# Feed-forward gate and up products by Strassen's algorithm in an fp32 streaming trunk: seven half-block products for eight

## The chip, the cores and the metric

The kernel runs on one core of one Trainium2 chip. The metric is device time of one execution in microseconds; the time given for a kernel is the median of its runs. The matmuls run on TensorE (PE; its weight loads are PEld), element-wise work on VectorE (DVE), ScalarE (ACT) and GpSimd (POOL), and SyncE (SP) issues the transfers that bring weights from DRAM.

## The reference

A two-layer trunk over 640 token columns (512 of a prompt, 8 x 16 of samples), width 1024, all in fp32. Each layer adds a mixer (pooling and differential attention in layer 0, an RWKV-7 recurrence in layer 1), cross-attention over a memory of 256 rows, and a gated feed-forward part of width 2816:

```python
def rmsnorm(x, g):
    y = x32 * lax.rsqrt(jnp.mean(x32 * x32, axis=-1, keepdims=True) + NORM_EPS)
    return y * g
def swiglu(h, wg, wu, wd):
    return (jax.nn.silu(h @ wg) * (h @ wu)) @ wd
...
x = x + swiglu(rmsnorm(x, P['norm_ffn_g'][l]), P['ffn_wg'][l], P['ffn_wu'][l], P['ffn_wd'][l])
```

The change is in the feed-forward part alone, in both layers.

## The kernel before

Activations stay in SBUF transposed: `x` is 8 blocks of 128 features by 640 tokens, and a product goes over the tokens in two halves of 320 (`HALVES`), one PSUM bank each. An fp32 product is made of three fp32r ones: each operand is split into a high part (rounded by a cast) and a low part (the rest), and `block_steps` issues wh·xh, wh·xl, wl·xh for each of the 8 feature blocks and both halves, 48 matmuls for one block of 128 outputs.

Weights are streamed. `load_w` brings one block (128 x 1024 numbers, 512 KB) into `wr` by a transfer on SP's queue; ACT casts it to `wh`, and DVE subtracts to get `wl`. Each of the three kinds has two buffers, taken in turn (`wtile`).

`ffn` works without the normalisation at first: `normed` splits x·gain, and the factor 1/rms of each token (`rstd`) comes in when a product leaves PSUM. So the first products start while `rms` is still squaring, summing (matmuls with `ones`), taking root and reciprocal, and spreading the factor over the partitions (matmuls with the diagonal `dg`). The 22 hidden blocks go in groups of 8, 8 and 6. For each block f: the gate product; DVE multiplies it by `rstd`, ACT takes Silu; the up product; DVE multiplies by `rstd`, POOL multiplies gate by up, and ACT and DVE split the result into `hid`. After a group, a pass over `wd` (8 blocks) adds its part to x. The products turn through banks 0 to 5; banks 6 and 7 serve `rms` and, at the end of layer 0, the transposes of the memory rows (`mem_parts`).

A scheduler orders the instructions of each engine at build time, with a timeline that it simulates; on the chip each engine works through its own list in that order, and waits at an instruction until its inputs and its output's buffer are free. SBUF is cut into 56 wide slots (`NSLOT`) and 22 narrow ones (`NHALF`); every temporary takes a slot from a free list and rotates over as many as its ring has.

Of the kernel before, what the change touches and what calls it, by code (L numbers as in the profile page):

```python
# [9 lines left out]
F32 = mybir.dt.float32  # L10
F32R = mybir.dt.float32r
AF = mybir.ActivationFunctionType
ALU = mybir.AluOpType
# [8 lines left out]
NT = NP + NB * TS  # L22
NF = 22
HALVES = ((0, 320), (320, 320))
NEG = -1.0e30
EPS = 1e-6
NSLOT = 56
NHALF = 22
NSMALL = 32


# [8 lines left out]
class Trunk:  # L40
# [21 lines left out]
    def __init__(self, ctx, tc, io):  # L62
# [5 lines left out]
        self.dr = ctx.enter_context(tc.tile_pool(name="dr", bufs=1, space=DRAM))  # L68
        self.free = {"t": deque(range(NSLOT)), "n": deque(range(NHALF))}
        self.scopes = [{}]  # L70
# [54 lines left out]
    def take(self, k, name, kind="t", dt=F32):  # L125
        h = Held()
        h.slots = [(kind, self.pop(kind, name)) for _ in range(k)]
        h.extend(self.slot(kind, i, name, dt) for _, i in h.slots)
        return h
# [102 lines left out]

    def wtile(self, kind, dt):
        i = self.turn[kind]
        self.turn[kind] = (i + 1) % 2
        return self.wp.tile([128, 1024], dt, tag=f"{kind}{i}", name=kind, bufs=1)

    def load_w(self, src, kb, cols, rows=128):
# [795 lines left out]


    def ffn(self, l):
        nc, io = self.nc, self.io
        self.banks(g=(0, 1, 2, 3, 4, 5), r=(6, 7))
        wg, wu, wd = io["ffn_wg"][l], io["ffn_wu"][l], io["ffn_wd"][l]
        hl = self.normed(self.col["norm_ffn_g"][:, 8 * l:8 * l + 8])  # L1040
        first = [[self.load_w(self.wview(w, 0, 8, 0, 128), 8, 128)] for w in (wg, wu)]
        _, rstd = self.rms("r")
        r0 = rstd[0]
        for f0, nf in ((0, 8), (8, 8), (16, 6)):
            hid = self.hl(nf, "hid")
            with self.scope():
                for f in range(nf):
                    g = self.t("gate")[:, 0:NT]
                    sg = self.t("sgate")[:, 0:NT]

                    def ev_g(m, pts):
                        for p, (t0, n) in zip(pts, HALVES):
                            self.tt(g[:, t0:t0 + n], p, r0[:, t0:t0 + n])
                            self.act(sg[:, t0:t0 + n], g[:, t0:t0 + n], AF.Silu)

                    def ev_u(m, pts):
                        for p, (t0, n) in zip(pts, HALVES):
                            self.tt(g[:, t0:t0 + n], p, r0[:, t0:t0 + n])
                            self.tt(g[:, t0:t0 + n], g[:, t0:t0 + n], sg[:, t0:t0 + n], eng=nc.gpsimd)
                            self.split((hid[f][0][:, t0:t0 + n], hid[f][1][:, t0:t0 + n]), g[:, t0:t0 + n])  # L1060

                    self.gemm(hl, wg, 128, ev_g, c0=(f0 + f) * 128, first=() if f0 + f else first[0])
                    self.gemm(hl, wu, 128, ev_u, c0=(f0 + f) * 128, first=() if f0 + f else first[1])
            if f0 == 16:
                self.give(hl, rstd)
                if l == 0:
                    self.mem = self.mem_parts("r")
            self.gemm(hid, wd, 1024, self.add_x, r0=f0 * 128)
            self.give(hid)


    def rwkv(self):
# [890 lines left out]
```

## Time and profile before

| | |
|---|---|
| median of 3 runs | 2404.35 us (2401.02 to 2410.25) |
| profiled execution, its own time | 2405.84 us |
| its span | 2403.7 us |
| mean granted TensorE clock | 0.961 |
| PE busy | 2248.9 us (94%) |
| DVE busy | 1259.0 us (52%) |
| ACT busy | 820.4 us (34%) |
| POOL busy | 455.6 us (19%) |

The page of the profile gives the busy time of each engine and its share of the span. The feed-forward parts run from about 562 to 1025 us and from 1921 to 2383 us. The trace can be asked for the busy time of engines in any stretch, for groups of instructions (busy time, count, mean of one, idle time before them), for waits, and for a timeline in which neighbouring instructions of one kind are drawn together with their count. In it DVE's splits, adds and products all stand at L211 (`tt`), the fused gain-and-factor product at L214 (`stt`), matmuls at L230 (`mm`).

### The profile page before, as it was taken

The page shows a single profiled execution, that of the slowest core. Times are in us where ns is not written, and L with a number is a line of the kernel's source. Part 1 is how long each engine was busy: PE and PEld are TensorE (multiplying, and loading weights), DVE is VectorE, ACT ScalarE, POOL GpSimd, SP SyncE. Part 2 cuts the span into 40 slices and gives each one's busy share as a digit, 9 for nine tenths or more (in the row PEclk, how much of TensorE's full clock was granted, in tenths as well). Part 3 has the DMA queues.
Part 4 walks back from the last instruction along what each step waited for, and adds up shares of the span by engine and source line. Part 5 has one row for each costly group of instructions (what it writes and reads, how often), then busy time and mean ns, then how long its engine had stood idle before and what let it go on. Part 6 is the DMA issues. An engine that isn't in the chain of part 4 may idle for free. (4 is left out here: it accounts for less than half of the span.)

```text
span 2403.7 us, 45518 instructions
## 1 busy us (share of the span) xinstructions
PE 2248.9 (94%) x18933; PEld 2098.5 (87%) x18933; DVE 1259.0 (52%) x2197; ACT 820.4 (34%) x1513; POOL 455.6 (19%) x480
## 2 busy tenths in 40 slices
PE   8998899999999999989998886885999999999998
PEld 7886799889999999988887875664998899999998
DVE  3566433445433434485758785589435544244344
ACT  4335332334222212366745432222323432122122
POOL 1113220002101101245433110233100211011010
PEclk9999999999999999999998987897999999999998
DMA  3228445533222222353236666673445222222222
GB/s 118 75 75 298 147 144 158 172 93 88 79 71 79 71 85 75 113 167 115 80 109 162 162 175 155 174 196 106 145 133 170 67 71 79 77 74 79 80 73 77
DMA packets 428063, 280.41 MB, mean 117 GB/s; under 512 B 78873, under 2 KB 383278, under 8 KB 427857
## 3 DMA queue, kind: packets, MB, share of 16 engines
q1 hardware_dynamic: 424257, 268.01, 38.3%
q0 software_dynamic: 3600, 9.49, 1.1%
q8 instruction: 149, 2.44, 0.4%
q14 instruction: 57, 0.47, 0.1%
HBM read 231.22 MB, written 46.20 MB: 115 GB/s over the span
## 5 line engine op out<-in xcount | busy, mean ns | idle before, releaser
L230 PE MATMUL p_g<-xn,wh 128*128 128x320 f32 x3712 | 719.4, 310 | 0.6 <-ACT wh L247 0.6
L230 PEld LDWEIGHTS p_g<-xn,wh 128*128 128x128 f32 x3712 | 588.5, 188 | 9.7 <-issue 8.4
L247 ACT CAST wh<-wr 128x1024 fp32r<-128x1024 f32 (+3 forms) x279 | 272.8, 979 | 854.7 <-PE p_g L230 512.0
L230 PE MATMUL p_g<-xn,wl 128*128 128x320 f32 x1856 | 443.1, 310 | 3.3 <-DVE wl L211 3.3
L211 DVE TENSOR_TENSOR wl<-wr,wh 128x1024 fp32r<-128x1024 f32 (+2 forms) x251 | 304.7, 1214 | 75.0 <-ACT wh L247 58.6
L230 PEld LDWEIGHTS p_g<-xn,wl 128*128 128x128 f32 x1856 | 315.3, 188 | 7.2 <-DVE wl L211 3.7
L230 PE MATMUL p_g<-hid,wh 128*128 128x320 f32 x1408 | 264.1, 309 | 0.0
L211 POOL TENSOR_TENSOR gate<-gate,sgate 128x320 f32<-128x320 f32 x88 | 118.0, 1362 | 726.9 <-DVE gate L211 726.9
L211 DVE TENSOR_TENSOR gate<-p_g,rstd 128x320 f32<-128x320 f32 x176 | 78.4, 487 | 326.7 <-PE p_g L230 324.0
L211 DVE TENSOR_TENSOR x<-x,p_g 128x320 f32<-128x320 f32 x192 | 85.5, 484 | 273.7 <-PE p_g L230 273.6
L230 PEld LDWEIGHTS p_g<-hid,wh 128*128 128x128 f32 x1408 | 220.8, 188 | 0.0
L230 PE MATMUL p_g<-hid,wl 128*128 128x320 f32 x704 | 160.8, 309 | 0.0
L230 PE MATMUL p_g<-mixr,wh 128*128 128x320 f32 (+2 forms) x640 | 132.9, 319 | 5.8 <-ACT wh L247 1.7
L230 PEld LDWEIGHTS p_g<-hid,wl 128*128 128x128 f32 x704 | 117.7, 188 | 0.0
L230 PEld LDWEIGHTS p_g<-mixr,wh 128*128 128x128 f32 (+2 forms) x640 | 101.3, 183 | 15.7 <-issue 5.9
L230 PE MATMUL p_g<-xohl,wh 128*128 128x320 f32 x512 | 110.2, 319 | 3.7 <-ACT xohl L220 3.6
L230 PEld LDWEIGHTS p_g<-xohl,wh 128*128 128x128 f32 x512 | 82.4, 188 | 8.9 <-ACT xohl L220 5.9
L230 PE MATMUL p_g<-mixr,wl 128*128 128x320 f32 (+2 forms) x320 | 79.8, 318 | 0.0
L211 POOL TENSOR_TENSOR acc<-acc,sq 128x640 f32<-128x640 f32 x30 | 52.9, 1764 | 140.4 <-ACT sq L208 140.4
L211 POOL TENSOR_TENSOR wl<-wr,wh 128x1024 fp32r<-128x1024 f32 (+2 forms) x28 | 65.3, 2333 | 73.1 <-ACT wh L247 71.8
L211 DVE TENSOR_TENSOR hid<-gate,hid 128x320 fp32r<-128x320 f32 x88 | 72.1, 819 | 7.7 <-ACT hid L220 7.7
L972 POOL TENSOR_SCALAR xp<-xp,xsm 128x256 f32<-128x256 f32 x32 | 15.3, 478 | 312.4 <-DVE xsm L708 300.8
(492 smaller groups left out, 3704.8 us busy)
## 6 DMA issues: line engine op xcount, KB each, us to landing
wr<-in_ffn_wg SPq DMA_DIRECT2D x44, 512.0 KB
wr<-in_ffn_wu SPq DMA_DIRECT2D x44, 512.0 KB
kc<-in_cache_mem_k SPq DMA_DIRECT2D x64, 256.0 KB
vc<-in_cache_mem_v SPq DMA_DIRECT2D x64, 256.0 KB
wr<-in_ffn_wd SPq DMA_DIRECT2D x32, 512.0 KB
wr<-in_ev_w_in SPq DMA_DIRECT2D x16, 512.0 KB
wr<-in_xa_wk SPq DMA_DIRECT2D x16, 512.0 KB
vc<-in_cache_diff_v SPq DMA_DIRECT2D x32, 256.0 KB
```

Of the source, the lines that this page charges most:

```text
L211: (eng or self.nc.vector).tensor_tensor(out, a, b, op=op)
L230: self.nc.tensor.matmul(out, lhsT, rhs, start=start, stop=stop, **kw)
L247: nc.scalar.copy(wh[0:rows, 0:n], wr[0:rows, 0:n])
L972: nc.gpsimd.tensor_scalar(p, p, rs, 1.0, op0=ALU.mult, op1=ALU.mult)
```

## The change

- The inputs are normalised before the first product: `ys` = x·gain·rstd is made for the 8 blocks by DVE (`stt`), then split into `xn`. PSUM results need no factor any more.
- Hidden blocks 0 to 3 are computed as before, with Silu taken by ACT straight from PSUM and gate times up by DVE; POOL has no part. Meanwhile DVE makes the operands T1 to T4 (differences of the four quarters: feature blocks 0-3 and 4-7, tokens 0-319 and 320-639) and they are split. Then comes a `wd` pass of four blocks.
- Hidden blocks 4 to 21 go in pairs through `strassen`, three groups of three pairs, each with a `wd` pass of six blocks. For a pair, gate and up are each a 2 x 2 product (two hidden blocks, two feature halves) times (two feature halves, two token halves). It is done by seven products in place of eight: three sums of raw weights before the split and one more after, S1 = A21+A22, S2 = S1-A11, A11-A21, A12-S2, by DVE. Each product has 2 x 4 x 3 = 24 matmuls of 320 columns and its own split of 128 x 1024 weights (one ACT cast, one DVE subtraction). Three products are summed up in the banks of role `a`, which are never reset between them; after some, ACT copies the running sum to SBUF (`take`), and DVE adds a product of role `b` to it (`out`), ACT takes Silu, DVE multiplies.
- Raw weights of a pair come in four tiles of 512 KB (the same bytes as before) into six tiles that rotate their roles from pair to pair. `wh` and `wl` have three buffers, `wr` two, everywhere in the kernel. There are 14 narrow slots for 22. The banks of products in `wd` passes are 4 to 7, shared with `mem_parts`.

```diff
@@ -25,7 +25,7 @@
 NEG = -1.0e30
 EPS = 1e-6
 NSLOT = 56
-NHALF = 22
+NHALF = 14
 NSMALL = 32


@@ -232,7 +232,7 @@

     def wtile(self, kind, dt):
         i = self.turn[kind]
-        self.turn[kind] = (i + 1) % 2
+        self.turn[kind] = (i + 1) % (2 if kind == "wr" else 3)
         return self.wp.tile([128, 1024], dt, tag=f"{kind}{i}", name=kind, bufs=1)

     def load_w(self, src, kb, cols, rows=128):
@@ -1034,39 +1034,147 @@


     def ffn(self, l):
         nc, io = self.nc, self.io
         self.banks(g=(0, 1, 2, 3, 4, 5), r=(6, 7))
         wg, wu, wd = io["ffn_wg"][l], io["ffn_wu"][l], io["ffn_wd"][l]
-        hl = self.normed(self.col["norm_ffn_g"][:, 8 * l:8 * l + 8])
+        gcol = self.col["norm_ffn_g"][:, 8 * l:8 * l + 8]
         first = [[self.load_w(self.wview(w, 0, 8, 0, 128), 8, 128)] for w in (wg, wu)]
         _, rstd = self.rms("r")
-        r0 = rstd[0]
-        for f0, nf in ((0, 8), (8, 8), (16, 6)):
+        ys = self.blocks(8, "xf")
+        hl = self.hl(8, "xn")
+        for k in range(8):
+            self.stt(ys[k], self.x[k], gcol[:, k:k + 1], rstd[0])
+            self.split(hl[k], ys[k])
+        self.give(rstd)
+        L, R = slice(0, 320), slice(320, 640)
+        c, d = self.hl(4, "xc"), self.hl(2, "xd")
+        with self.scope():
+            hid = self.hl(4, "hid")
+            for f in range(4):
+                sg, pr = self.t("sgate")[:, 0:NT], self.t("gate")[:, 0:NT]
+                def ev_g(m, pts):
+                    for p, (t0, n) in zip(pts, HALVES):
+                        self.act(sg[:, t0:t0 + n], p, AF.Silu)
+                def ev_u(m, pts):
+                    for p, (t0, n) in zip(pts, HALVES):
+                        self.tt(pr[:, t0:t0 + n], p, sg[:, t0:t0 + n])
+                    self.split(hid[f], pr)
+                self.gemm(hl, wg, 128, ev_g, c0=f * 128, first=() if f else first[0])
+                self.gemm(hl, wu, 128, ev_u, c0=f * 128, first=() if f else first[1])
+                if f == 1:
+                    for k in range(4):
+                        y1, y2 = ys[k], ys[4 + k]
+                        self.tt(y1[:, L], y1[:, R], y1[:, L], ALU.subtract)
+                        self.tt(y1[:, R], y2[:, R], y1[:, R], ALU.subtract)
+                        self.tt(y2[:, R], y2[:, R], y1[:, L], ALU.subtract)
+                        self.tt(y2[:, L], y2[:, L], y2[:, R], ALU.subtract)
+                        self.split(c[k], y2)
+                        self.split([t[:, (L, R)[k % 2]] for t in d[k // 2]], y1[:, R])
+        for k in range(4):
+            self.split((hl[k][0][:, R], hl[k][1][:, R]), ys[k][:, L])
+        self.give(ys)
+        self.gemm(hid, wd, 1024, self.add_x)
+        self.give(hid)
+        part = lambda h, s: (h[0][:, s], h[1][:, s])
+        rhs = dict(B11=[part(hl[k], L) for k in range(4)], T1=[part(hl[k], R) for k in range(4)],
+                   B21=[part(hl[4 + k], L) for k in range(4)], B22=[part(hl[4 + k], R) for k in range(4)],
+                   T2=[part(c[k], R) for k in range(4)], T3=[part(d[k // 2], (L, R)[k % 2]) for k in range(4)],
+                   T4=[part(c[k], L) for k in range(4)])
+        for f0, nf in ((4, 6), (10, 6), (16, 6)):
+            self.banks(a=(0, 1, 2, 3), b=(4, 5, 6, 7), g=(4, 5, 6, 7), r=(6, 7))
             hid = self.hl(nf, "hid")
+            at = dict(A11=0, A21=1, A22=2, A12=3, S1=4, S2=5)
             with self.scope():
-                for f in range(nf):
-                    g = self.t("gate")[:, 0:NT]
-                    sg = self.t("sgate")[:, 0:NT]
-
-                    def ev_g(m, pts):
-                        for p, (t0, n) in zip(pts, HALVES):
-                            self.tt(g[:, t0:t0 + n], p, r0[:, t0:t0 + n])
-                            self.act(sg[:, t0:t0 + n], g[:, t0:t0 + n], AF.Silu)
-
-                    def ev_u(m, pts):
-                        for p, (t0, n) in zip(pts, HALVES):
-                            self.tt(g[:, t0:t0 + n], p, r0[:, t0:t0 + n])
-                            self.tt(g[:, t0:t0 + n], g[:, t0:t0 + n], sg[:, t0:t0 + n], eng=nc.gpsimd)
-                            self.split((hid[f][0][:, t0:t0 + n], hid[f][1][:, t0:t0 + n]), g[:, t0:t0 + n])
-
-                    self.gemm(hl, wg, 128, ev_g, c0=(f0 + f) * 128, first=() if f0 + f else first[0])
-                    self.gemm(hl, wu, 128, ev_u, c0=(f0 + f) * 128, first=() if f0 + f else first[1])
+                for f in range(0, nf, 2):
+                    self.strassen(wg, wu, f0 + f, rhs, hid[f:f + 2], at)
+                    at = dict(A21=at["A11"], A22=at["S2"], A11=at["S1"], A12=at["A21"], S1=at["A12"], S2=at["A22"])
             if f0 == 16:
-                self.give(hl, rstd)
+                self.give(hl, c, d)
                 if l == 0:
                     self.mem = self.mem_parts("r")
             self.gemm(hid, wd, 1024, self.add_x, r0=f0 * 128)
             self.give(hid)
+    def strassen(self, wg, wu, f, rhs, hid, at):
+        nc = self.nc
+        L, R = slice(0, 320), slice(320, 640)
+        def raw(nm):
+            i = at[nm]
+            if i < 4:
+                return self.wide(("zr0", "zr1", "bk0", "bk1")[i], "wraw")[:, 0:1024]
+            return self.wp.tile([128, 1024], F32, tag=f"wr{i - 4}", name="wraw", bufs=1)
+        A = {}
+        for nm, fi, kh in (("A21", 1, 0), ("A22", 1, 1), ("A11", 0, 0), ("A12", 0, 1)):
+            A[nm] = raw(nm)
+            for i, w in enumerate((wg, wu)):
+                nc.sync.dma_start(out=A[nm][:, 512 * i:512 * i + 512].rearrange("p (k m) -> p k m", k=4),
+                                  in_=self.wview(w, 512 * kh, 4, (f + fi) * 128, 128))
+        def parts(t):
+            hi, lo = self.wtile("wh", F32R), self.wtile("wl", F32R)
+            self.split((hi, lo), t)
+            return [w.rearrange("p (i k m) -> p i k m", i=2, k=4) for w in (hi, lo)]
+        def product(pts, w, x, start):
+            for i, p in enumerate(pts):
+                n = 0
+                for k in range(4):
+                    for a, b in ((0, 0), (0, 1), (1, 0)):
+                        self.mm(p[:, 0:320], w[a][:, i, k, :], rhs[x][k][b], start=start and n == 0, stop=n == 11, skip_group_check=True)
+                        n += 1
+        def take(pts, i, s):
+            for p, t in zip(pts, tmp[i]):
+                nc.scalar.copy(t[:, s], p[:, 0:320])
+        def out(i, s, pts=None, direct=False):
+            tg, tu = [t[:, s] for t in tmp[i]]
+            if direct:
+                self.act(tg, pts[0][:, 0:320], AF.Silu)
+                self.tt(pr[i][:, s], pts[1][:, 0:320], tg)
+                return
+            self.tt(tg, tg, pts[0][:, 0:320], ALU.add)
+            self.act(tg, tg, AF.Silu)
+            self.tt(tu, tu, pts[1][:, 0:320], ALU.add)
+            self.tt(pr[i][:, s], tu, tg)
+        tmp = [[self.t(f"e{i}{j}", 1)[:, 0:NT] for j in range(2)] for i in range(2)]
+        pr = [self.t(f"gate{i}", 1)[:, 0:NT] for i in range(2)]
+        S1, S2 = raw("S1"), raw("S2")
+        self.tt(S1, A["A21"], A["A22"], ALU.add)
+        self.tt(S2, S1, A["A11"], ALU.subtract)
+        self.tt(A["A21"], A["A11"], A["A21"], ALU.subtract)
+        pa = [self.ps("a") for _ in range(2)]
+        product(pa, parts(A["A11"]), "B11", True)
+        take(pa, 0, L)
+        pb = [self.ps("b") for _ in range(2)]
+        product(pb, parts(A["A12"]), "B21", True)
+        out(0, L, pb)
+        product(pa, parts(S2), "T2", False)
+        take(pa, 1, L)
+        self.tt(A["A12"], A["A12"], S2, ALU.subtract)
+        product(pa, parts(S1), "T1", False)
+        take(pa, 1, R)
+        pc = [self.ps("b") for _ in range(2)]
+        product(pc, parts(A["A21"]), "T3", True)
+        out(1, R, pc)
+        product(pa, parts(A["A12"]), "B22", False)
+        out(0, R, pa, True)
+        self.split(hid[0], pr[0])
+        product(pc, parts(A["A22"]), "T4", False)
+        out(1, L, pc)
+        self.split(hid[1], pr[1])


     def rwkv(self):
```

The scheduler's order for the changed kernel, read from the two programs: first DVE where the feed-forward part of layer 0 starts. Before (xn is x·gain, dg the diagonal, p_r the bank of the spread factor):

```order
L214 SCALAR_TENSOR_TENSOR xn<-x,ct,xn 128x640
L211 TENSOR_TENSOR acc<-acc,sq 128x640
L211 TENSOR_TENSOR wl<-wr,wh 128x1024
L512 RECIPROCAL rtok<-rtok 128x5
L211 TENSOR_TENSOR dg<-ident,rtok 128x640
L200 COPY rstd<-p_r 128x320
L211 TENSOR_TENSOR gate<-p_g,rstd 128x320 x4
L211 TENSOR_TENSOR wl<-wr,wh 128x1024
L211 TENSOR_TENSOR hid<-gate,hid 128x320 x2
```

Now (xf is `ys`, xn its split; rows with a count stand for so many in a row):

```order
L211 TENSOR_TENSOR wl<-wr,wh 128x1024
L211 TENSOR_TENSOR acc<-acc,sq 128x640
L512 RECIPROCAL rtok<-rtok 128x5
L211 TENSOR_TENSOR dg<-ident,rtok 128x640
L200 COPY rstd<-p_r 128x320
L214 SCALAR_TENSOR_TENSOR xf<-x,ct,rstd 128x640 x8
L211 TENSOR_TENSOR xn<-xf,xn 128x640 x7
L211 TENSOR_TENSOR xf<-xf 128x320
L211 TENSOR_TENSOR xn<-xf,xn 128x640
L211 TENSOR_TENSOR xf<-xf 128x320 x9
L211 TENSOR_TENSOR xd<-xf,xd 128x320
L211 TENSOR_TENSOR xf<-xf 128x320
```

The eight products with the factor stand ahead of the first subtraction of a split, and the first differences for T1 to T4 ahead of the next weight's subtraction; the results of the first gate product were DVE's next work before.

ACT at the same place, before:

```order
L208 ACTIVATE xn<-x,ct 128x640
L208 ACTIVATE sq<-x 128x640
L247 CAST wh<-wr 128x1024
L208 ACTIVATE xn<-x,ct 128x640
L208 ACTIVATE sq<-x 128x640
L247 CAST wh<-wr 128x1024
L208 ACT_TABLE_LOAD
L208 ACTIVATE rtok<-p_r,epsc 128x5
L198 COPY rstd<-p_r 128x320
L208 ACT_TABLE_LOAD
L208 ACTIVATE sgate<-gate 128x320 x2
L247 CAST wh<-wr 128x1024
```

And now:

```order
L247 CAST wh<-wr 128x1024
L208 ACTIVATE sq<-x 128x640
L247 CAST wh<-wr 128x1024
L208 ACTIVATE sq<-x 128x640
L247 CAST wh<-wr 128x1024
L208 ACTIVATE sq<-x 128x640
L208 ACT_TABLE_LOAD
L208 ACTIVATE rtok<-p_r,epsc 128x5
L198 COPY rstd<-p_r 128x320
L220 CAST xn<-xf 128x640 x8
L220 CAST xd<-xf 128x320 x4
L247 CAST wh<-wr 128x1024
```

A cast of a third weight block now stands ahead of the last square (`sq`), and eight casts of `xn` follow the factor's copy. On TensorE nothing stands any more between the last product of cross-attention and the `rms` matmuls (`ones`, then `dg`); behind them come six matmuls of three weight blocks with the high part of `xn`'s first block, and the first matmul with a low part.

Then one pair in the middle of a group, around its last three products. DVE before, one hidden block:

```order
L211 TENSOR_TENSOR gate<-p_g,rstd 128x320 x2
L211 TENSOR_TENSOR wl<-wr,wh 128x1024
L211 TENSOR_TENSOR gate<-p_g,rstd 128x320 x2
L211 TENSOR_TENSOR wl<-wr,wh 128x1024
L211 TENSOR_TENSOR hid<-gate,hid 128x320 x2
```

DVE now (e_7342 and e_7343 are the gate and up sums of the pair's second block, wraw raw weights, p_b the banks of the T3 and T4 products):

```order
L211 TENSOR_TENSOR wl<-wraw,wh 128x1024
L211 TENSOR_TENSOR gate_7344<-e_7341,e_7340 128x320
L211 TENSOR_TENSOR wl<-wraw,wh 128x1024
L211 TENSOR_TENSOR wraw<-wraw 128x1024
L211 TENSOR_TENSOR e_7342<-e_7342,p_b 128x320
L211 TENSOR_TENSOR wraw<-wraw 128x1024
L211 TENSOR_TENSOR wl<-wraw,wh 128x1024
L211 TENSOR_TENSOR e_7343<-e_7343,p_b 128x320
L211 TENSOR_TENSOR wl<-wraw,wh 128x1024
```

ACT now, at the same pair (L1138 is `take`, in the changed kernel's lines):

```order
L1138 COPY e_7342<-p_a 128x320
L220 CAST wh<-wraw 128x1024
L1138 COPY e_7343<-p_a 128x320
L1138 COPY e_7342<-p_a 128x320
L208 ACTIVATE e_7342<-e_7342 128x320
L220 CAST wh<-wraw 128x1024
L1138 COPY e_7343<-p_a 128x320
L220 CAST wh<-wraw 128x1024
```

In a pair the cast of the last weight tile (A22) stands behind the Silu of the T3 result, and its subtraction behind the addition of that result and a sum of the next pair's raw weights; before, a block's subtractions stood between results that were read from PSUM.

## Rows read from the trace of the kernel before

**Rows 1.** The page, busy time of the engines: us, share of the span, instructions.

```profile
PE 2248.9 (94%) x18933; PEld 2098.5 (87%) x18933; DVE 1259.0 (52%) x2197; ACT 820.4 (34%) x1513; POOL 455.6 (19%) x480
```

**Rows 2.** Windows over both feed-forward parts: stretch, length, busy us (count), clock, DMA share, GB/s.

```profile
562.00:1025.00 463.00, 463.00 (x3172) 462.64 (x3171) 188.73 (x260) 117.68 (x176) 69.10 (x58) 1.00 0.28 82
1921.00:2383.00 462.00, 462.00 (x3163) 461.68 (x3162) 186.92 (x252) 109.39 (x161) 59.76 (x45) 1.00 0.26 75
```

**Rows 3.** Timeline around 1033 us: start, us, engine, line, operation.

```profile
1032.58 0.40 PE L230 MATMUL p_g<-memhl,wh 128*128 128x256 f32 x2
1032.81 0.28 PE L230 MATMUL p_g<-memhl,wl 128*128 128x256 f32 x1
...
1032.93 0.40 PE L230 MATMUL p_g<-memhl,wh 128*128 128x256 f32 x2
```

**Rows 4.** Timeline, start of layer 0's feed-forward part.

```profile
561.12 0.37 SPq L245 DMA_DIRECT2D wr<-in_ffn_wg  x1
...
562.33 0.75 PE L230 MATMUL p_g<-xn,wh 128*128 128x320 f32 x4
...
564.04 0.72 ACT L208 ACTIVATE sq<-x 128x640 f32<-128x640 f32 x1
...
565.30 0.82 DVE L211 TENSOR_TENSOR acc<-acc,sq 128x640 f32<-128x640 f32 x1
...
569.19 1.17 PE L230 MATMUL p_r<-ones,acc 128*128 128x1 f32 x10
...
571.64 0.27 ACT L208 ACTIVATE rtok<-p_r,epsc 128x5 f32<-128x5 f32 x1
...
572.17 0.82 DVE L211 TENSOR_TENSOR dg<-ident,rtok 128x640 f32<-128x640 f32 x1
...
575.86 1.24 PE L230 MATMUL p_r<-dg,ones 128*128 128x320 f32 x4
...
577.13 0.43 ACT L198 COPY rstd<-p_r 128x320 f32<-128x320 f32 x1 [5.22 <-PE p_r L230]
```

**Rows 5.** Windows across the landing of that weight block.

```profile
563.50:564.00 0.50, 0.50 (x6) 0.50 (x5) 0.50 (x1) 0.50 (x1) 0.00 (x0) 1.00 1.13 343
564.00:564.50 0.50, 0.50 (x5) 0.50 (x4) 0.50 (x1) 0.50 (x2) 0.00 (x0) 1.00 0.29 83
```

**Rows 6.** DVE groups from 500 to 562 us: count, busy us, mean ns, idle before.

```profile
L214 DVE SCALAR_TENSOR_TENSOR xn<-x,ct,xn 128x640 fp32r<-128x640 f32 x7 | 6.1, 882 | 0.7 <-ACT xn L208 0.6
...
L211 DVE TENSOR_TENSOR wl<-wr,wh 128x1024 fp32r<-128x1024 f32 x1 | 1.2, 1226 | 0.1
```

**Rows 7.** Windows after layer 0's feed-forward part, where TensorE paused.

```profile
1048.00:1050.00 2.00, 0.00 (x0) 0.00 (x0) 2.00 (x5) 1.03 (x1) 1.96 (x4) 1.00 0.00 0
...
1052.00:1054.00 2.00, 2.00 (x14) 1.25 (x12) 2.00 (x5) 1.30 (x2) 1.28 (x3) 0.50 0.04 9
1054.00:1056.00 2.00, 2.00 (x14) 1.78 (x14) 2.00 (x5) 1.28 (x3) 1.43 (x3) 0.50 0.60 184
1056.00:1058.00 2.00, 2.00 (x17) 1.67 (x14) 1.87 (x3) 1.85 (x4) 2.00 (x1) 0.80 0.58 121
```

**Rows 8.** DVE groups of layer 0's feed-forward part.

```profile
L211 DVE TENSOR_TENSOR wl<-wr,wh 128x1024 fp32r<-128x1024 f32 x59 | 80.9, 1371 | 7.8 <-ACT wh L247 5.3
L211 DVE TENSOR_TENSOR gate<-p_g,rstd 128x320 f32<-128x320 f32 x88 | 39.2, 487 | 163.3 <-PE p_g L230 162.0 <-ACT sgate L208 1.3
...
L211 DVE TENSOR_TENSOR memhl<-p_r,memhl 128x256 fp32r<-128x256 f32 x8 | 3.3, 419 | 7.4 <-ACT memhl L220 7.4
```

**Rows 9.** ACT groups of the same stretch.

```profile
L247 ACT CAST wh<-wr 128x1024 fp32r<-128x1024 f32 x60 | 63.2, 1053 | 269.5 <-PE p_g L230 163.9 <-issue 105.6
...
L220 ACT CAST memhl<-p_r 128x256 fp32r<-128x256 f32 x8 | 2.8, 373 | 7.4 <-PE p_r L227 7.4
```

**Rows 10.** TensorE's waits over the whole span: us in total, times, longest.

```profile
PE p_g L230 <- DVE wl L211: 8.0, 11, 3.3
...
PE p_g L230 <- ACT wh L247: 5.9, 4, 2.6
```

## The prediction, made before the changed kernel was run

> **What bounds the kernel now.** I read the page's busy times first [rows 1]: TensorE works 94% of the span, the others at most half. [...] The working goes by the profiled execution, 2405.84 us, which is 1.5 above the median of the runs.
>
> **Matmuls removed.** Gate and up of one layer take 22 x 2 x 48 = 2112 matmuls. Now four blocks take 4 x 96 = 384, and nine pairs 9 x 7 x 24 = 1512: 1896, or 216 fewer. Two layers: 432 x 0.146 = 63.1 us less. The products of `strassen` fill one bank with 12 matmuls in a row where before two banks took turns. That costs nothing: products of the memory rows do it too, and three of 256 columns start 0.35 us apart (1032.58 to 1032.93) [rows 3], 0.117 each, which is 256/320 of 0.146. The `wd` passes have as many matmuls as before, in four passes for three; each has its weights ahead in the order, so I take nothing for the fourth.
>
> **The start, which now waits for the norm.** Before, TensorE goes straight from cross-attention into the feed-forward products at 562.33, and the chain of `rms` runs beside them until 577.56 [rows 4]. Now it must run first. I walk it in layer 0:
> - The first weight block is issued at 561.12 [rows 4] and has landed at about 564.2, where the DMA share falls from 1.13 to 0.29 [rows 5]. In ACT's new order a cast stands ahead of the last square, and it needs a third load; I take this landing for it. Cast 1.05 [rows 9]: 565.25. Square 0.72 [rows 4]: 565.97.
> - DVE has that block's subtraction first, 1.23 [rows 6], from 565.25 to 566.48, then adds the square, 0.82 [rows 4]: 567.3.
> - Ten matmuls with `ones` took 1.17 [rows 4]. TensorE has been idle for 5 us by then; I take 1.7: 569.0. Root, reciprocal and diagonal took from 571.64 to 572.99 [rows 4], 1.35: 570.35. The `dg` matmuls and the copies took from 575.86 to 577.56 [rows 4], 1.70; I take 2.5 at a lower clock: 572.85.
> - Eight products with the factor stand ahead of the first subtraction, each 0.882 [rows 6]: 7.06, to 579.9. The subtraction, priced as the addition of the same shape, 0.82 [rows 4]: 580.7.
>
> TensorE is held from 562.33 to 580.7, 18.4 us. Two things come off: the 2.4 us of `rms` matmuls (1.17 + 1.24 [rows 4]), which interrupted the products before and lie in the pause now, and six matmuls that need high parts only, 0.9. Seven further subtractions come every 0.82 us, and with three weight blocks in flight a block of `xn` feeds 18 matmuls, 2.6 us: no further wait. [...] So 18.4 - 2.4 - 0.9 + 2.4 = 17.5 per layer. Layer 1 has the same order: +35 us. Ends: if the clock stays up and the short matmuls keep their old times, 2.4 + 1.3 less, 27.6; if the load is the third of a queue and one block takes 3.1 us (561.12 to 564.2), 3.1 more is possible in each layer, or the low level lasts longer: 43.
>
> [...]
>
> **The pairs.** TensorE needs 168 x 0.146 = 24.5 us for a pair. DVE: seven subtractions at 1.23 [rows 6]; four sums of raw weights, same shape and price; ten operations of 320 columns at 0.49 [rows 8]; two `hid` subtractions at 0.82: 8.6 + 4.9 + 4.9 + 1.6 = 20.0 us. ACT: seven casts at 1.05 [rows 9], ten copies and Silus at 0.43 [rows 4], two casts at 0.72: 13.1. Both fit, DVE at 82%; but queues are in order. The narrowest place is the last tile, A22. Its cast stands behind the Silu of the T3 result, and its subtraction behind that cast: from the end of the T3 product 0.49 (addition) + 0.43 + 1.05 + 1.23 = 3.2 us. TensorE has the next product meanwhile, 24 x 0.146 = 3.5, and meets the low part 0.3 us into A22's: 0.6 us to spare. The raw tiles land 3.1 us after issue and rotate over six. I take no stall: 0. Upper end: 1.5 us in each of 18 pairs, 27.
>
> [...] A subtraction does take 1.371 on average beside POOL's gate product [rows 8] and 1.226 before it [rows 6]. POOL has no work in pairs, hence 1.23; at 1.371 DVE would be at 21.6 us, still within 24.5.
>
> **The memory rows.** In layer 0 their transposes now share banks 6 and 7 with the last `wd` pass. Eight splits read them, 0.37 on ACT and 0.42 on DVE each [rows 8, 9]: 6.3 us if TensorE waits for each, 0 if for none. I take 3.
>
> **Everywhere else** the third `wh` and `wl` buffer and 14 narrow slots change only the order. At most the third buffer takes away all of TensorE's waits for `wl` and `wh`, 8.0 + 5.9 = 13.9 [rows 10]; at the other end the new order in the recurrence may cost as much. I take 0.
>
> **The sum:** 2405.84 - 63.1 + 35 + 3 = 2380.7, and 1.5 less for the median of the runs: about 2380 us.
>
> **Rivals.**
> - *Queues hold TensorE in each pair; slower.* If the Silu of T3 comes later than I think (a sum of raw weights of 1.2 us that slips ahead of the addition is enough), A22's cast and subtraction, 1.05 + 1.23 = 2.3 us, lie bare: 18 x 2.3 = 41, so about 2421. It speaks for it that 0.6 us is all there is; against it, that the order has a second pair's work to slide. It makes the change worthless from (63.1 - 38)/18 = 1.4 us per pair. Chance 0.13.
> - *A shorter start.* The third load is early and the clock stays at the upper level: 12 us per layer, 24: about 2369; with the gain of the third buffer 2360. Chance 0.14.
> - *No change.* Loss in the rest (fewer slots, another order in the recurrence) of 13.9, or a start at its upper end with the memory rows at theirs (8 + 3): 2391 to 2405 together, say 2398. Chance 0.11.
> - *My forecast*, with its own range 2368 to 2392: 0.62.
>
> **How the numbers follow.** Half a per cent, 12 us, is what a measurement of this kernel can tell from no change: faster means below 2392. That holds for the forecast (0.62 less its tail of 0.04), the shorter start (0.14) and a little of the third: 0.73. Same, to 2416: most of the third, the forecast's tail and a mild form of the first: 0.15. Slower: 0.12. The range 2358 to 2404 takes in the shorter start and the lower half of no change, and leaves the first rival out.
>
> **What would show it.** In the profile after: about 2956 matmuls (3172 - 216) in a feed-forward part of some 449 us (463 - 31.5 + 17.5); TensorE idle once, 15 to 20 us, at each start, with a granted clock of 0.50 behind it; no wait of TensorE for `wl` or `wh` over 0.3 us within pairs; DVE near 80% there, and its subtraction at 1.23. I am wrong if TensorE waits for A22's parts pair after pair, if the matmuls of `strassen` take more than 0.146, if the pause is far from 17 us, or if the rest of the program moves by more than 10 us.

## The result, and the profile after

The changed kernel takes 2371.46 us, the median of 4 runs (2366.8 to 2379.64), where the kernel before takes 2402.68 in the same set: a ratio of 0.9868, with a 95% interval of 0.9831 to 0.9905. The prediction was 2380, with 2368 to 2392 as the likeliest case's own range. The profiled execution took 2374.25 us, its span is 2372.5.

The page of the changed kernel, busy time of the engines; TensorE has 432 matmuls less than before [rows 1], DVE and ACT have more to do:

```profile
PE 2204.5 (93%) x18501; PEld 2053.0 (87%) x18501; DVE 1402.2 (59%) x2419; ACT 924.0 (39%) x1671; POOL 337.3 (14%) x392
```

Windows of the changed kernel over its two feed-forward parts (stretch, length, busy us and count of each engine, granted clock, DMA share, GB/s):

```profile
563.00:1020.00 457.00, 444.38 (x2983) 441.49 (x2982) 270.66 (x379) 175.73 (x263) 13.92 (x17) 0.98 0.27 81
1904.00:2353.00 449.00, 439.04 (x2962) 437.23 (x2963) 264.82 (x369) 166.28 (x246) 0.00 (x0) 0.98 0.24 71
```

Before, TensorE was busy all the time at clock 1.00 [rows 2]. Now it is idle for some 12.6 and 10.0 us, and the clock is 0.98. All of TensorE's waits in the first of these parts (us in total, times, longest):

```profile
PE p_r L230 <- DVE acc L211: 3.7, 1, 3.7
PE p_g L230 <- DVE xn L211: 3.6, 1, 3.6
PE p_g L230 <- ACT xn L220: 2.2, 1, 2.2
PE p_r L230 <- DVE dg L211: 1.4, 1, 1.4
PE p_r L227 <- DVE memhl L211: 0.9, 1, 0.9
PE p_g L230 <- DVE memhl L211: 0.8, 1, 0.8
```

Four waits belong to the start, two to the memory rows. There is none for `wl`, `wh` or a sum of raw weights: in nine pairs TensorE never waits. The start itself stands in the chain of work from 560 to 585 us (start, us, what):

```profile
560.01 3.69 DMA wr<-in_ffn_wg
...
563.78 1.05 ACT wh L247
...
564.86 0.66 DVE wl L211
...
566.00 0.83 DVE acc L211
...
566.87 1.93 PE p_r L230 x10
...
568.82 0.28 ACT rtok L208
...
569.34 0.84 DVE dg L211
...
570.22 2.52 PE p_r L230 x4
...
572.76 0.43 ACT rstd L198
...
573.22 2.51 DVE xf L214 x4
...
576.41 3.27 DVE xf L214 x4
579.68 0.75 DVE xn L211
```

This is the walk of the prediction, link by link: the load, the cast ahead of the last square, the subtraction ahead of the addition (which [rows 4] had at 565.30), ten matmuls with `ones`, the diagonal, the spread factor, eight products, then the first subtraction. TensorE's rows at its end (start, us, idle time before and what ended it):

```profile
574.92 1.97 PE L230 MATMUL p_g<-xn,wh 128*128 128x320 f32 x6 [2.19 <-ACT xn L220]
580.47 0.90 PE L230 MATMUL p_g<-xn,wh 128*128 128x320 f32 x2 [3.58 <-DVE xn L211]
```

The last matmul of cross-attention ends its turn at 563.02, so TensorE is held for 17.4 us; 18.4 was forecast. In layer 1 it is 16.0: the cast ahead of the last square starts there at 1903.65, 0.1 us before cross-attention ends, and waits for no load.

How the span divides (from the end of the last cross-attention matmul to the end of the last matmul on `hid`, each read from the timeline):

| us | start to first part | first part | between | second part | tail | span |
|---|---|---|---|---|---|---|
| before | 562.3 | 467.1 | 891.3 | 465.2 | 17.8 | 2403.7 |
| changed | 563.0 | 457.3 | 883.5 | 450.0 | 18.8 | 2372.5 |
| difference | +0.7 | -9.8 | -7.8 | -15.2 | +1.0 | -31.2 |

The feed-forward parts give 25.0 us, where the prediction's sum had 25.1. The other 6 come from stages whose source did not change.

### The profile page after: what moved, and what is told of

It reads as the page before. It is cut to its first block, busy times and chain, and to the rows that moved or that the text cites. A ratio compares the mean times of both kernels' runs of the same rounds, so it can differ in the third digit from the quotient of the medians.

```text
span 2372.5 us, 45267 instructions
## 1 busy us (share of the span) xinstructions
PE 2204.5 (93%) x18501; PEld 2053.0 (87%) x18501; DVE 1402.2 (59%) x2419; ACT 924.0 (39%) x1671; POOL 337.3 (14%) x392
## 4 chain that ended last, share of the span: by engine, by line
PE 77%; DVE 8%; DMA 7%; ACT 3%; SPq 3%; issue 2%; POOL 0%; DVEq 0%; ACTq 0%; POOLq 0%
PE p_g L230 45%; PE p_a L230 11%; PE p_b L230 8%; PE p_s L230 3%; PE p_o L230 2%; PE p_k L227 2%; SPq L1678 1%; PE p_y L230 1%; DVE wl L211 1%; PE p_x L230 1%; DMA d_bt<-am 1%; PE p_t L227 1%; DVE yl L211 1%; PE p_f L230 1%; ACT wh L247 1%
## 5 line engine op out<-in xcount | busy, mean ns | idle before, releaser
L230 PE MATMUL p_g<-xn,wh 128*128 128x320 f32 x1408 | 295.0, 318 | 11.9 <-DVE xn L211 7.2
L211 DVE TENSOR_TENSOR wl<-wr,wh 128x1024 fp32r<-128x1024 f32 (+2 forms) x195 | 201.0, 1031 | 96.3 <-ACT wh L247 85.1
L230 PEld LDWEIGHTS p_g<-xn,wh 128*128 128x128 f32 x1408 | 231.9, 193 | 23.3 <-issue 8.4
L211 DVE TENSOR_TENSOR wl<-wraw,wh 128x1024 fp32r<-128x1024 f32 x126 | 154.1, 1223 | 107.6 <-ACT wh L220 76.3
L220 ACT CAST wh<-wraw 128x1024 fp32r<-128x1024 f32 x126 | 132.5, 1051 | 164.6 <-PE p_a L230 79.1
L230 PE MATMUL p_a<-xn,wh 128*128 128x320 f32 x864 | 190.9, 308 | 0.0
L230 PE MATMUL p_g<-xn,wl 128*128 128x320 f32 x704 | 183.1, 315 | 4.8 <-DVE wl L211 4.8
L230 PEld LDWEIGHTS p_a<-xn,wh 128*128 128x128 f32 x864 | 144.4, 188 | 0.0
L230 PE MATMUL p_a<-xn,wl 128*128 128x320 f32 x432 | 132.7, 308 | 0.0
L230 PEld LDWEIGHTS p_g<-xn,wl 128*128 128x128 f32 x704 | 124.7, 192 | 8.8 <-DVE wl L211 5.2
```

The source lines that it names most:

```text
L211: (eng or self.nc.vector).tensor_tensor(out, a, b, op=op)
L220: self.nc.scalar.copy(hi, src)
L230: self.nc.tensor.matmul(out, lhsT, rhs, start=start, stop=stop, **kw)
```

## The experiments

Each row of the table at the end of this section has a kernel's stages. A total moves with the middle stage too, so each theory is judged by the stage it speaks of.

**Fourteen narrow slots alone.** In the kernel before:

```diff
-NHALF = 22
+NHALF = 14
```

> The kernel before with 14 narrow slots for 22 and nothing else. The changed kernel took 7.8 us less than before between the two feed-forward parts (891.3 us before, 883.5 after). If the third weight buffer did that, this kernel stays at about 2403 us. If the smaller set of slots, through another order, did it, it comes to about 2396 us. Feed-forward parts 467 and 465 us by either.

It measured 2409.98 us (ratio 1.0025, 1.0014 to 1.0036): neither number. The parts stay at 467.1 and 465.2, the middle is 894.5. The slots by themselves do not bring the 7.8 us.

**The third buffer alone**, with the same slots:

```diff
-        self.turn[kind] = (i + 1) % 2
+        self.turn[kind] = (i + 1) % (2 if kind == "wr" else 3)
```

> The kernel before with three wh and wl buffers and 14 narrow slots. If the third buffer makes the 7.8 us outside the feed-forward parts: about 2396 us, with TensorE's waits for wl and wh (8.0 and 5.9 us before) smaller. If those 7.8 us come from the scheduler's other order and not from the buffer: anywhere between 2390 and 2415 us, and the waits for wl and wh stay. Feed-forward parts 467 and 465 us.

It measured 2417.18 us (1.0058, 1.0037 to 1.0079), above what either case expected. TensorE's waits for `wl` and `wh` did shrink, against [rows 10]; the rows of this kernel over its whole span:

```profile
PE p_g L230 <- DVE wl L211: 5.7, 4, 2.9
...
PE p_g L230 <- ACT wh L247: 2.9, 2, 2.2
```

That is 5.3 us less waiting, and yet the middle stage grew by 8.4 and the first part by 3.3. So this build waits less for the two and is still 7.2 us slower than the one with 14 slots alone; whether the buffer or the new order does that, these two runs cannot tell. And in the changed kernel, whose middle is shorter, the two waits are not smaller than before:

```profile
PE p_g L230 <- DVE wl L211: 8.4, 5, 4.8
...
PE p_g L230 <- ACT wh L247: 6.6, 3, 4.0
```

**Normalised first, eight products.** The changed kernel with the loop of plain blocks over all 22 (groups of 8, 8 and 6, without T1 to T4):

```diff
-        for f0, nf in ((4, 6), (10, 6), (16, 6)):
...
-                    self.strassen(wg, wu, f0 + f, rhs, hid[f:f + 2], at)
+        for f0, nf in ((0, 8), (8, 8), (16, 6)):
...
+                    self.gemm(hl, wg, 128, ev_g, c0=(f0 + f) * 128, first=() if f0 + f else first[0])
+                    self.gemm(hl, wu, 128, ev_u, c0=(f0 + f) * 128, first=() if f0 + f else first[1])
```

> The changed kernel with the plain eight products for all 22 hidden blocks: inputs normalised first and third buffer stay, Strassen is gone. If the start costs what the chain of the prediction says, 17.5 us per layer: feed-forward parts of about 484 and 482 us, 432 matmuls x 0.146 = 63 us more than the changed kernel, less 3 us of memory rows: about 2431 us. Rival: the pairs themselves lose time that the prediction did not see and the start is cheaper; then the parts are shorter than 478 us and the total is below 2420 us.

The parts are 484.5 and 482.2 us, as expected: normalising first costs 17.4 and 17.1 us against the kernel before. All waits of TensorE in the first of them belong to the start:

```profile
PE p_g L230 <- DVE xn L211: 3.6, 1, 3.6
PE p_r L230 <- DVE acc L211: 3.3, 1, 3.3
PE p_g L230 <- ACT xn L220: 2.2, 1, 2.2
PE p_r L230 <- DVE dg L211: 1.4, 1, 1.4
```

Against the changed kernel, Strassen's products save 27.3 and 32.3, 59.6 together; 63.1 less 3 for the memory rows were forecast. The total of 2444.24 is above the expected 2431, because the middle came out at 894.1.

**The factor late.** The first four blocks as before, with `rstd` at the eviction; the normalised operands are made meanwhile and put into `xn` behind the fourth block:

```diff
+        hl = self.normed(gcol)
...
+                        self.tt(pr[:, t0:t0 + n], p, r0[:, t0:t0 + n])
+                        self.act(sg[:, t0:t0 + n], pr[:, t0:t0 + n], AF.Silu)
...
+        for k in range(8):
+            self.split(hl[k], ys[k])
+        self.give(ys, rstd)
         self.gemm(hid, wd, 1024, self.add_x)
```

> Strassen's pairs stay, but the first four blocks use inputs without the factor, as the kernel before did, and the factor comes in when a product leaves PSUM; the normalised operands are made beside these four blocks. If the start is the cost (17 us per layer), it is gone: feed-forward parts of about 439 and 434 us, total about 2338 us. Rival: DVE has now 8 more products of 640 columns, 16 evictions and 8 splits ahead of the first pair, and holds TensorE there by 10 us or more per layer: 2360 us or more.

It measured 2349.87 us (0.9779, 0.9759 to 0.98). The parts are 440.2 and 435.9, 17.1 and 14.1 less than the changed kernel's. All waits of TensorE in its first part:

```profile
PE p_r L227 <- DVE memhl L211: 0.9, 1, 0.9
PE p_g L230 <- DVE memhl L211: 0.8, 1, 0.8
PE p_g L230 <- DVE xn L214: 0.5, 1, 0.5
PE p_g L230 <- ACT xn L208: 0.3, 1, 0.3
```

The start is gone, and DVE's added work holds nothing: the rival falls. The total is 12 us above the 2338 expected, since the middle took 891.0, not the changed kernel's 883.5, and the parts are 1 to 2 us longer.

**Two weight buffers.** The changed kernel with

```diff
-        self.turn[kind] = (i + 1) % (2 if kind == "wr" else 3)
+        self.turn[kind] = (i + 1) % 2
```

> The changed kernel with two wh and wl buffers for three. If two are enough in a pair (a cast and a subtraction, 2.3 us, go beside one product of 3.5 us): feed-forward parts within 5 us of 457 and 450, and the total differs from the changed kernel's 2371 us only by what the order of the rest does, up to 15 us either way. If the third buffer is what keeps the pairs fed: TensorE waits up to 2.3 us in each of 18 pairs, parts of up to 478 and 471 us, total up to 2412 us.

The parts are 455.2 and 452.7: two buffers feed the pairs, with two waits of TensorE in them, 1.7 us together. But the total is 2405.58 us, as long as before (1.0016, 0.9999 to 1.0033): the middle took 913.0, more than the 15 us either way that I had allowed.

**More work for DVE in each pair.** Three extra sums, which write S1 again (and six, with `range(7)`):

```diff
-        self.tt(S1, A["A21"], A["A22"], ALU.add)
+        for _ in range(4):
+            self.tt(S1, A["A21"], A["A22"], ALU.add)
```

> The changed kernel with the sum S1 made four times in each pair, three more DVE instructions of 1.22 us (the result is the same). DVE's work in a pair grows from 20.0 to 23.7 us of TensorE's 24.5. By busy time alone nothing changes: feed-forward parts of 457 and 450 us. By queues in order, the three stand in front of subtractions that TensorE waits for: 1 to 3.7 us per pair, 9 to 33 us in each part.

> The same with six more, 27.3 us of DVE work against 24.5 of TensorE: DVE bounds the pair. At least 2.8 us per pair, 25 us in each part: 482 and 475 us, total 2421 us or more. If TensorE's time hid DVE further, less than 10 us in each part.

With three, nothing changes: parts of 457.6 and 449.8, total 2370.76. A stretch of pairs and `wd` passes in the changed kernel:

```profile
700.00:960.00 260.00, 260.00 (x1775) 260.00 (x1774) 161.20 (x211) 103.68 (x152) 1.17 (x1) 1.00 0.27 80
```

and with the three sums:

```profile
700.00:960.00 260.00, 260.00 (x1775) 260.00 (x1774) 187.28 (x238) 103.59 (x153) 1.16 (x1) 1.00 0.28 81
```

DVE works 26 us more and TensorE issues the same 1775 matmuls. In the fullest pair (693.1 to 717.8 us) DVE is busy 23.4 of 24.7 us. With six, the parts grow by 30.4 and 31.6 us, 3.4 per pair, and the total is 2445.46 us; TensorE's longest wait in this kernel is now

```profile
PE p_a L230 <- DVE wl L211: 27.9, 12, 2.4
```

DVE is not full on the average: from 720 to 980 us it is busy 188.00 us, hardly more than with three. But its work comes in runs. Windows of this kernel around a wait of 2.38 us for `wl` at 700.53:

```profile
690.00:702.00 12.00, 9.42 (x59) 8.64 (x58) 11.98 (x16) 5.07 (x8) 0.00 (x0) 0.97 0.33 93
702.00:706.00 4.00, 4.00 (x21) 4.00 (x20) 0.01 (x1) 1.28 (x2) 0.00 (x0) 0.65 0.86 251
```

DVE works without a break up to 702 and its subtraction comes late; then it is idle for 4 us, with ACT busy for 1.28 of them (by my reading ACT's next cast waits for TensorE in its turn), and the granted clock falls to a mean of 0.65 besides. So, by the prediction's sums, 23.7 us of DVE work are hidden beside a pair's 24.5 us of TensorE and 27.3 are not. Where between them it breaks, and how much of the 62 us is the order of the queues and the clock (the waits for `wl` are 27.9), is not shown.

**Matmuls in the pause.** The changed kernel with 12 matmuls that nothing reads ahead of the `rms` ones and 28 behind:

```diff
+        self.keep(12)
         _, rstd = self.rms("r")
+        self.keep(28)
...
+    def keep(self, n):
+        p = self.ps("r")
+        for _ in range(n):
+            self.mm(p[:, 0:128], self.ident, self.ones, start=True, stop=True, skip_group_check=True)
```

> The changed kernel with 12 and 28 extra matmuls of 128 columns, which nothing reads, in the two pauses at the start of each feed-forward part. If TensorE's granted clock falls because it pauses, it stays at 1.00 there: the dg matmuls take 1.24 us for 2.50, the ones matmuls 1.17, the first products run at 0.146 us each, and each part is 3 to 4 us shorter: 453.5 and 446.5 us. If the clock falls for another reason, the granted clock at the start is 0.50 as without them, and the parts stay at 457 and 450 us or grow by the extra matmuls.

The parts are 455.9 and 447.1, 1.3 and 2.8 less, where 3 to 4 were expected. Windows of the changed kernel at the start:

```profile
566.00:568.00 2.00, 1.13 (x7) 1.13 (x8) 0.82 (x2) 0.76 (x1) 0.00 (x0) 0.83 0.21 62
568.00:570.00 2.00, 0.78 (x4) 0.70 (x4) 0.85 (x2) 0.27 (x1) 0.00 (x0) 0.50 0.67 200
...
582.00:584.00 2.00, 2.00 (x9) 2.00 (x9) 2.00 (x3) 0.00 (x0) 0.00 (x0) 0.50 0.00 0
```

and with the extra matmuls:

```profile
566.00:568.00 2.00, 0.47 (x5) 0.41 (x4) 1.02 (x2) 0.27 (x1) 0.00 (x0) 0.77 0.71 207
568.00:570.00 2.00, 2.00 (x4) 1.16 (x5) 0.49 (x1) 0.00 (x0) 0.00 (x0) 0.50 0.03 8
...
572.00:574.00 2.00, 2.00 (x12) 2.00 (x11) 2.00 (x3) 1.86 (x3) 0.00 (x0) 0.52 0.00 0
574.00:576.00 2.00, 2.00 (x20) 2.00 (x20) 2.00 (x4) 1.79 (x4) 0.00 (x0) 1.00 0.00 0
```

The clock fell in both, around 567 us: during the `ones` matmuls of the changed kernel, and between those and the ones with `dg` here; the latter take 2.5 us either way. The twelve in front did not hold it. While the 28 behind ran it came back, at 574, ahead of the products; without them it stayed at 0.50 until 584. So with matmuls in the second pause the products start at 1.00, without them at 0.50. Why the twelve in front did not keep the clock at 1.00, these runs do not show. The total, 2381.92, is 10 us above the changed kernel's: the middle took 898.6.

**High parts first.** The matmuls of the first four products in another order:

```diff
+        if self.hi_first:
+            seq = [(a, hl[k][0], k) for k in range(kb) for a in (wh, wl)] + [(wh, hl[k][1], k) for k in range(kb)]
```

> The changed kernel with the matmuls of the first four products in another order: for all eight blocks those with the high part of the inputs first, then those with the low part. The subtractions at the start are then needed later, and TensorE's wait of 3.6 us for xn's low part goes; part of the clock's loss too. Feed-forward parts 452 and 445 us, 5 us less each. If the casts feed TensorE no faster than the subtractions did, it waits for eight casts instead, and the parts stay at 457 and 450 us. The total goes with the draw of the order besides.

The parts are 451.8 and 444.4, 5.5 less each. The wait for xn's low part, 3.6 us, is gone; the other three at the start are left (a line lower in this kernel). The clock is back 4.1 us after the first product and not 9.5, which is part of the other 1.9 us:

```profile
PE p_r L231 <- DVE acc L212: 4.1, 1, 4.1
PE p_g L231 <- ACT xn L221: 2.2, 1, 2.2
PE p_r L231 <- DVE dg L212: 1.4, 1, 1.4
```

The total is 2371.33, since the middle took 892.5.

**The same instructions in other slots.** The changed kernel, and the late one, with

```diff
         self.ffn(0)
+        self.free["t"].rotate(7)
         self.rwkv()
```

> The changed kernel with the list of free slots turned by seven between the first feed-forward part and the recurrence: the same instructions, only other slots for the temporaries from there on, and so another order from the scheduler. If the 883.5 us between the feed-forward parts are one draw among many orders (880 to 913 us in the kernels run so far), this stage changes by several us while the first feed-forward part stays at 457: a total between 2368 and 2402 us. If the stage is set by what the change does to buffers, it stays at 883 and the total at 2371 us, within 3.

> The kernel with the late factor and the same turn of the free list. Feed-forward parts 440 and 436 us as without it. If the stage between them is a draw of the order, a total between 2339 and 2372 us; if not, 2350 us.

The changed kernel becomes 2391.25 us (0.9958, 0.9943 to 0.9973): the first part stays at 457.5 and the middle goes from 883.5 to 899.1. The late one becomes 2340.03 (0.9747, 0.9729 to 0.9765): parts 440.0 and 435.2, middle 880.7. The middle goes up in one kernel and down in the other, by the same turn of a list. Its core is the recurrence, taken here from the last matmul `p_g<-mixr,wh` to the last transpose of `yl`. Windows over it in the kernel before,

```profile
1280.00:1676.00 396.00, 310.14 (x4837) 263.68 (x4837) 302.32 (x591) 133.25 (x298) 91.61 (x110) 0.82 0.63 164
```

in the changed kernel,

```profile
1267.40:1662.80 395.40, 318.45 (x4855) 270.65 (x4854) 295.35 (x592) 131.90 (x296) 91.16 (x109) 0.82 0.67 172
```

in the changed kernel with other slots,

```profile
1268.80:1674.70 405.90, 319.01 (x4846) 269.94 (x4845) 300.03 (x592) 131.91 (x296) 89.79 (x109) 0.81 0.65 167
```

in the one with two buffers,

```profile
1272.60:1684.90 412.30, 319.55 (x4848) 271.21 (x4846) 299.49 (x590) 132.41 (x298) 93.83 (x110) 0.81 0.63 163
```

and in the late one with other slots:

```profile
1244.60:1638.90 394.30, 319.52 (x4856) 271.32 (x4855) 296.54 (x592) 131.43 (x296) 89.79 (x109) 0.82 0.67 170
```

DVE and ACT are busy for the same 300 and 132 us within 2%, and the stage takes 394 to 412. No engine is busy throughout, so the difference lies in who waits for whom. The changed kernel's own 7.8 us are not made here: its recurrence takes 395.4 us, 0.6 less than before. They lie ahead of it (247.1 us for 250.6) and behind it (241.0 for 244.7).

**Late factor, two buffers, 22 narrow slots.**

> The late factor with two wh and wl buffers and 22 narrow slots, as in the kernel before. If two buffers feed the pairs, as they did in the changed kernel (455 and 453 us), the feed-forward parts stay within 4 us of 440 and 436, and the total is between 2339 and 2372 us by the draw of the order. If the third buffer helps at the start, where three blocks are in flight, the parts are longer by 5 us or more.

It measured 2356.13 us (0.9812, 0.9792 to 0.9832); parts 440.6 and 437.1: the third buffer is not needed at the start either. The middle took 897.2.

| kernel | first part | between | second part | median | ratio |
|---|---|---|---|---|---|
| before | 467.1 | 891.3 | 465.2 | 2402.7 | |
| changed | 457.3 | 883.5 | 450.0 | 2371.5 | 0.9868 |
| 14 slots | 467.1 | 894.5 | 465.2 | 2410.0 | 1.0025 |
| third buffer | 470.3 | 899.7 | 465.4 | 2417.2 | 1.0058 |
| normalised, 8 products | 484.5 | 894.1 | 482.2 | 2444.2 | 1.017 |
| late factor | 440.2 | 891.0 | 435.9 | 2349.9 | 0.9779 |
| Strassen, 2 buffers | 455.2 | 913.0 | 452.7 | 2405.6 | 1.0016 |
| 3 more sums | 457.6 | 879.9 | 449.8 | 2370.8 | 0.9868 |
| 6 more sums | 487.7 | 898.9 | 481.5 | 2445.5 | 1.0174 |
| matmuls in the pause | 455.9 | 898.6 | 447.1 | 2381.9 | 0.9917 |
| high parts first | 451.8 | 892.5 | 444.4 | 2371.3 | 0.9878 |
| other slots | 457.5 | 899.1 | 451.6 | 2391.3 | 0.9958 |
| late, other slots | 440.0 | 880.7 | 435.2 | 2340.0 | 0.9747 |
| late, 2 buffers, 22 slots | 440.6 | 897.2 | 437.1 | 2356.1 | 0.9812 |

The stages are those of one profiled execution each. The runs of one kernel spread by 0.5 to 22 us, so differences of a few us in the middle are not told apart; 880 and 913 are. The ten builds with 14 slots and three buffers lie between 879.9 and 899.7; of the four with two buffers one is at 913.0.

## Why the prediction was right, point by point

- *Matmuls removed, -63.1.* Right: with eight products the two parts are 59.6 us longer, and with the memory rows' 3 off, 60.1 were forecast. The 0.146 us of the sum is 463.00 / 3172 of [rows 2], and pairs and `wd` passes run at the same (260 us / 1775).
- *The start, +35.* Right: 34.5 us between the kernel before and the one that normalises first and keeps eight products (it has the changed kernel's buffers and slots, too). In layer 0 the chain ends at 580.47 for 580.7; TensorE is held 17.4 us for 18.4 mainly because cross-attention ended 0.7 us later. The eight products follow each other every 0.81 us and not 0.88, but the `dg` matmuls and the copies took 3.0 us and not 2.5. Two terms were off, and cancel in part in layer 0 alone: the `rms` matmuls held the products of the kernel before for 1.0 and 0.8 us (from their start to the next product's, 569.19 to 570.22 and 575.86 to 576.69), not for 2.4; and the sum's 2.4 us for the clock was an estimate that no run shows. What showed in its place: the granted clock was still 0.50 for the first 3.9 us after 580.47 in layer 0 and the first 6.1 after 1919.70 in layer 1; 14 and 22 matmuls of 320 columns started there every 0.279 and 0.275 us and not every 0.146, so 1.9 and 2.8 us were lost. The late factor takes 31 us of the start back.
- *The pairs, 0.* Right, with room: no wait in them, none with three sums more; DVE is busy 20.5 of 24.6 us in the fullest pair (690.5 to 715.1 us). The 0.6 us that I gave A22 was too pessimistic: the scheduler lets matmuls of two products alternate. Here the last product (p_b<-xc) starts at 709.82, but matmuls on p_a stand between that and its first low part at 712.32:

```profile
709.75 1.22 DVE L211 TENSOR_TENSOR wl<-wraw,wh 128x1024 fp32r<-128x1024 f32 x1
...
709.82 0.45 PE L230 MATMUL p_b<-xc,wh 128*128 128x320 f32 x2
...
712.32 0.32 PE L230 MATMUL p_b<-xc,wl 128*128 128x320 f32 x1
```

  The last subtraction ahead of that ends at 710.97, so at least 1.3 us were to spare.

  DVE's price without POOL's work, 1.223 us per subtraction (group of the changed kernel from 700 to 970 us), was the 1.226 of [rows 6]:

```profile
L211 DVE TENSOR_TENSOR wl<-wraw,wh 128x1024 fp32r<-128x1024 f32 x51 | 62.4, 1223 | 45.2 <-ACT wh L220 30.3 <-PE p_b L230 13.8
```

- *The memory rows, +3.* Somewhat more: against the kernel with eight products layer 0 gained 5.0 us less than layer 1 (27.3 and 32.3), and the memory rows are the work that only layer 0 has. Two waits show, 1.7 us; the granted clock about them, 0.86 from 980 to 990 us and 0.97 in the next ten, loses about as much again, which was not in the forecast.
- *Everywhere else, 0, between -13.9 and as much above.* The step that was off. The changed kernel got -6, which is most of the 8.5 us between forecast and result, and not for the reason that I gave for the lower end: its waits for `wl` and `wh` did not shrink. In the other nine builds with three buffers these waits are 7.2 to 11.9 us together, in the four with two buffers 13.6 to 17.3; so the buffer does take some away, but the middle stages of the two sets overlap (879.9 to 899.7 and 891.3 to 913.0). Turning the free list, with the same instructions, moves the middle by +15.6 and -10.2, more than the 6 in question. So the -6 is within what the scheduler's order alone can make. With the changed kernel's slots and buffers the draws lie between -11 and +8 about the kernel before, within the range that I gave; the +22 of the build with two buffers lies outside it, and no run tells its order from its buffers. With the draw of the turned list the changed kernel takes 2391.25 us, 11 above the forecast. The forecast of the sign was right by the feed-forward parts; how near the total came was partly luck. (In the rival of a shorter start, 2369 less all of the 13.9 is 2355, not 2360.)

What stays open: why one order of the stages between is better (the waits are spread over many instructions, and no run here tells which of them starts the others), and what the third buffer is worth there on the average of many orders.

## What to carry to other kernels

Where TensorE was busy throughout a stage, fewer matmuls paid at their full price (59.6 us for 60.1), and DVE's added work cost nothing while it fitted beside TensorE's (23.7 us beside 24.5 cost nothing, 27.3 cost 3.4 per pair, though DVE was idle at times). Before a value is moved ahead of the first product, walk the chain that now has to run first: here it gave back more than half of the gain, and applying the factor late for four blocks got it back (2349.87 us, and 2340.03 in the best order, for 2371.46). And where a scheduler sets the order, an edit redraws stages it never touches: compare stage by stage, and turn an idle choice such as the slots to learn how wide that draw is before crediting a few tenths of a per cent to anything.

## What was not expected of the hardware

With twelve matmuls of 128 columns (2.94 us of work) in front of the pause, TensorE's granted clock still fell to 0.50, 2.5 us after they had ended, while it worked in short pieces with gaps of 0.5 and 1.5 us; it came back at 574, while 28 more ran in a row from 570.1. The other surprise is no hardware: 20 us between the best and the worst middle stage of ten builds with the same slots, buffers and source for that stage.
